# An encoder kernel of two batches: the SBUF slots of each size in pools of their own, at multiples of 256 bytes or more

## The chip, the cores and the metric

The kernel runs on one core of one Trainium2 chip. Its engines are TensorE (PE in the profile, with PEld for the loading of its weights), VectorE (DVE), ScalarE (ACT), GpSimd (POOL) and SyncE (SP), which here issues DMAs. SBUF is the memory on the core, 128 partitions side by side; an address below is a byte offset within a partition, the same in all of them. The metric is the device time of one execution in microseconds, the median of several runs.

## The reference

One layer of an encoder runs over two batches of rows, `x_prompt` (512 rows) and `x_sample` (1024 rows) of 1024 channels, with the same weights, all in float32:

```
h = rmsnorm(x);  z = h @ w_in                       # 1024 x 1792: q, k, v, two conv halves
A = windowed attention(q, k, v)                      # 8 heads of 64, 2 for k and v, |q - k| <= 128, bias, sink
c = ca * sigmoid(cb);  c = dwconv31(c);  c = silu(layernorm(c))
x = x + concat(A, c) @ w_out                         # 1024 x 1024
h = rmsnorm(x);  u = dwconv3(h @ w_up)               # 1024 x 5632
x = x + (silu(u[:, :2816]) * u[:, 2816:]) @ w_down   # 2816 x 1024
y = rmsnorm(x)
```

The outputs are `y_prompt` and `y_sample`, float32.

## The kernel before

Every float32 product is made of fp32r matmuls. An operand is split into a high part (a copy rounded to fp32r, on ACT) and a low part (the operand less the high part, on POOL or DVE), and a product adds three matmuls: high by high, high by low and low by high. Nearly all of them have 128x128 weights and 512 moving columns, so that the moving operand is 2048 bytes in each partition and the weights are 512.

The stages follow each other: transposes and the combined projection (`proj`, lines L299, L300 and L302, one for each of the three matmuls of a product), with the 31-tap convolution beside it on DVE (L354), then attention (L575 for the scores), the output projection, and from about 790 us on the gated MLP for both batches at once. Its up projection and its down projection each save products by a scheme with seven in place of eight, which adds and subtracts blocks ahead of them. The up projection is `prod` (L1079, L1080, L1081), the down projection `mm_down` (L1413, L1414, L1415). The order of instructions on SP and PE is written out by hand in the last part and set by a scheduler before that; no part of it depends on addresses.

All working tiles lie in slots. `Slots` is given classes of slots by a letter: 15 `q` slots of 4096 bytes, 61 `h` of 2048, 4 `c` of 4224, 2 `d` of 2176 and 32 `s` of 64. A request takes the first free slot of the smallest class that fits and gives it back when its tile goes. Where no slot under 4096 bytes is free, a `q` slot is cut into two halves. A slot is a tag of the tile pool `big`: the pool gives a tag its place in SBUF when the tag is first used, and the size that the first tile of the tag has, a multiple of 32 bytes. So the slots lie in the order of their first use, and the sizes are mixed. A second `Slots`, `raws` (L1018), holds the raw weights of the up projection in `q` slots that the first one has handed over.

Where the slots begin in the program as it is built:

```
before   q0 20640, q1 to q5 24736 to 41120, q6 to q14 86432 to 119200
         h0 18592, h1 45280, h2 47392, h3 49504, h4 to h20 51616 to 84384,
         h21 to h27 123296 to 135584, h28 to h32 139808 to 148000, h33 150112, h34 152224, h35 154336,
         h36 to h53 158624 to 193440, h54 195552, h55 197664, h56 199776, h57 to h60 201888 to 208032
         d0 137632, d1 156384, c0 210272, c1 214560, c2 218784, c3 223008
```

Modulo 256, all `q` slots begin at 160, of the `h` slots 48 at 160, h1, h35 and h54 at 224, h2, h28 to h32 and h55 at 32, and h3, h33 and h56 at 96, d0 at 160 and d1 at 224, c0 at 96, c1 and c3 at 32 and c2 at 160. Every slot begins at 32 or 96 past a multiple of 128. Parts of a slot that a matmul reads begin at multiples of 512 bytes within it, so they keep the slot's place modulo 256, the one that the prediction calls an operand's place. Of the 6196 fp32r matmuls, 4416 have weights and moving operand both at 160, and 1780 have one of the two (or both) at 32, 96 or 224. The constants, among them the identity matrix for the transposes, lie in a pool of their own ahead of the slots.

The slots are set up in these lines, which the change replaces or extends:

```
big = ctx.enter_context(tc.tile_pool(name="big", bufs=1))
sb = Slots(big, dict(q=(15, 4096), c=(4, 4224), h=(61, 2048), d=(2, 2176), s=(32, 64)), "q", KEEP)
raws = Slots(big, {})
```

Of the kernel before, what the change touches and what calls it, by code (L numbers as in the profile page):

```python
# [9 lines left out]
F32 = mybir.dt.float32  # L10
# [5 lines left out]
P = 128  # L16
# [40 lines left out]
KEEP = 3  # L57
# [3 lines left out]
U0 = 2  # L61


class Slots:


# [10 lines left out]
    def tile(self, shape, dt=F32, nbytes=4, among=None):  # L77
        need = nbytes
        for s in shape:
            need *= s  # L80
        fits = [s for s in self.free if s[1] >= need and (among is None or s[0][0] in among)]
        if self.halved and nbytes == 4 and need <= 2048 and not any(s[1] < 4096 for s in fits):
            halves = self.halves[dt]
            if not halves and sum(s[0][0] == self.halved for s in fits) > self.keep:
                slot = next(s for s in fits if s[0][0] == self.halved)
                self.free.remove(slot)
                self.n += 1
                whole = Whole(self, slot, dt, self.pool.tile([P, 2, 512], dt, tag=slot[0], name=f"{slot[0]}_{self.n}", bufs=1))
                halves += [(whole, 0), (whole, 1)]
                whole = None  # L90
            if halves:
                return Half(*halves.pop(0), shape)
        if not fits:
            raise RuntimeError(f"no slot for {need} bytes")
        least = min(s[1] for s in fits)
        slot = next(s for s in fits if s[1] == least)
        self.free.remove(slot)
        self.n += 1
        return Held(self, slot, (self.pool(slot[0]) if callable(self.pool) else self.pool).tile([P] + list(shape), dt, tag=slot[0], name=f"{slot[0]}_{self.n}", bufs=1))
# [46 lines left out]
def tile_hybrid_encoder(ctx: ExitStack, tc: tile.TileContext, xs, rel_bias, norm_attn_g, w_in,  # L146
                        attn_sink, conv_dw_w, conv_dw_b, conv_ln_g, conv_ln_b, w_out, norm_ffn_g,
                        w_up, ffn_dw_w, ffn_dw_b, w_down, norm_final_g, onehot, outs):
    nc = tc.nc
    cst = ctx.enter_context(tc.tile_pool(name="cst", bufs=1))  # L150
    big = ctx.enter_context(tc.tile_pool(name="big", bufs=1))
    dr = ctx.enter_context(tc.tile_pool(name="dr", bufs=1, space=bass.MemoryType.DRAM))
    ps_guards = [tc.tile_pool(name=f"ps{i}", bufs=1, space=bass.MemoryType.PSUM) for i in range(4)]
    ps = [guard.__enter__() for guard in ps_guards]
    two_of = dict(a0=0, a1=0, a2=1, u0=1, u1=2, b0=2, b1=3, c0=3)

    sb = Slots(big, dict(q=(15, 4096), c=(4, 4224), h=(61, 2048), d=(2, 2176), s=(32, 64)), "q", KEEP)
    banks = Slots(lambda tag: ps[two_of[tag]], dict(a=(3, 2048), u=(2, 2048), b=(2, 2048), c=(1, 2048)))
    use = dict(step="aub", turn="aub", conv="c", attn="au", norm="b", out="b", up="u", down="b")

# [43 lines left out]
    raws, ws = {}, {}  # L204
# [810 lines left out]


    uraw, third_sum, ops, done = {}, {}, {}, set()
    raws = Slots(big, {})  # L1018

    def reserve(n):  # L1020
        for slot in [s for s in sb.free if s[0][0] == "q"][:n]:
# [636 lines left out]
```

## Time and profile before

| | |
|---|---|
| median of 3 runs | 1562.92 us (1562.15 to 1564.94) |
| profiled execution, from its first to its last instruction | 1559.5 us |
| granted clock of TensorE, mean | 0.990 |
| PE busy | 1505.8 us, 6843 matmuls |
| PEld busy | 1228.9 us |
| DVE busy | 1126.9 us |
| ACT busy | 795.2 us |
| POOL busy | 709.7 us |
| moved by DMA | 227.17 MB, 45.6% of the 16 DMA engines' time |

The page gives the profiled execution's span and no other time of its own. A matmul's duration in the profile runs from its start to the end of its last column's way through the array, so that it is longer than the distance to the start of the next one, and a busy PE is not the same as a PE at its peak. How fast PE goes is read from the distance between starts. In names such as `w<-h,q` the letters are the slot classes: a result in a PSUM bank called `w` from a moving operand in an `h` slot and weights in a `q` slot, or in half of one.

### The profile page before, as it was taken

To read this page: it belongs to the slowest core of one execution; us is meant where nothing else is said; L and a number is where in the kernel's file an instruction comes from. 1 tells how busy PE (TensorE), PEld (TensorE's weight loads), DVE (VectorE), ACT (ScalarE), POOL (GpSimd) and SP (SyncE) were. 2 spreads that over 40 slices of the span, in tenths; PEclk is the share of its full clock that TensorE was granted. 3 is DMA by queue.
4 is the path that set the end of the run, shared out by engine and by line. 5 is a ranking of instruction groups with operands and counts; after the bars stand their busy time and mean duration, and the time that the engine had idled before them with its cause. 6 is when DMAs were issued, how large, how long until landed. Compare 5 with 4: busy or idle time off the path is not lost. (4 is left out here: it accounts for less than half of the span.)

```text
span 1559.5 us, 20112 instructions
## 1 busy us (share of the span) xinstructions
PE 1505.8 (97%) x6843; PEld 1228.9 (79%) x6843; DVE 1126.9 (72%) x1604; ACT 795.2 (51%) x1404; POOL 709.7 (46%) x566
## 2 busy tenths in 40 slices
PE   8998998899999999899999999999999999999997
PEld 6787787787888888777777888888888788888885
DVE  7999767858789785334868777777776845569883
ACT  4634654335787786623455445554545543444354
POOL 6652343226666775947434555555544000003355
PEclk9999999899999999999999999999999999999999
DMA  7582334447344346779332333333332582357644
GB/s 229 157 212 78 108 99 124 128 131 226 111 132 130 117 130 182 241 235 305 108 95 75 102 101 102 102 102 102 102 115 75 191 280 82 105 166 233 220 132 162
DMA packets 228780, 227.17 MB, mean 146 GB/s; under 512 B 13268, under 2 KB 168348, under 8 KB 228549
## 3 DMA queue, kind: packets, MB, share of 16 engines
q1 hardware_dynamic: 228677, 225.88, 45.6%
q8 instruction: 54, 0.88, 0.2%
q14 instruction: 49, 0.40, 0.1%
HBM read 164.74 MB, written 62.14 MB: 145 GB/s over the span
## 5 line engine op out<-in xcount | busy, mean ns | idle before, releaser
L193 POOL TENSOR_TENSOR q<-q,q 128x1024 fp32r<-128x1024 f32 x72 | 173.3, 2414 | 93.5 <-ACT q L192 36.7
L955 POOL TENSOR_TENSOR q<-q,q 128x512 fp32r<-128x512 f32 x101 | 140.7, 1398 | 163.8 <-ACT q L1065 151.5
L955 DVE TENSOR_TENSOR h<-h,h 128x512 fp32r<-128x512 f32 (+2 forms) x202 | 158.4, 817 | 66.2 <-ACT h L959 26.1
L1413 PE MATMUL w<-h,h 128*128 128x512 f32 x462 | 181.4, 393 | 0.5 <-DVE q L1200 0.5
L1414 PE MATMUL w<-h,h 128*128 128x512 f32 x462 | 181.5, 393 | 0.0
L1415 PE MATMUL w<-h,h 128*128 128x512 f32 x462 | 181.1, 392 | 0.0
L1079 PE MATMUL w<-h,q 128*128 128x512 f32 x448 | 176.4, 394 | 3.0 <-ACT w L1171 1.6
L1081 PE MATMUL w<-h,q 128*128 128x512 f32 x448 | 175.5, 392 | 1.0 <-POOL q L955 1.0
L1080 PE MATMUL w<-h,q 128*128 128x512 f32 x426 | 166.5, 391 | 0.0
L299 PE MATMUL u<-h,q 128*128 128x512 f32 x400 | 161.1, 403 | 5.0 <-DVE h L852 4.2
L300 PE MATMUL u<-h,q 128*128 128x512 f32 x400 | 158.9, 398 | 0.0
L302 PE MATMUL u<-h,q 128*128 128x512 f32 x384 | 152.2, 396 | 2.7 <-POOL q L193 2.7
L952 POOL TENSOR_TENSOR q<-q,q 128x1024 f32<-128x1024 f32 x12 | 33.1, 2769 | 238.1 <-DMA h<-gb 197.4
L354 DVE SCALAR_TENSOR_TENSOR c<-c,cvw,c 128x512 f32<-128x512 f32 x184 | 137.9, 750 | 2.9
L959 ACT CAST h<-h 128x512 fp32r<-128x512 f32 x120 | 71.8, 619 | 95.9 <-DVE h L955 42.5
L299 PE MATMUL b<-h,q 128*128 128x512 f32 x256 | 102.3, 400 | 2.7 <-DVE d L384 1.9
L1413 PEld LDWEIGHTS w<-h,h 128*128 128x128 f32 x462 | 86.8, 188 | 20.7 <-ACT h L959 0.9
L1415 PEld LDWEIGHTS w<-h,h 128*128 128x128 f32 x462 | 86.7, 188 | 19.7
L852 DVE SCALAR_TENSOR_TENSOR h<-u,fw,h 128x511 f32<-128x511 f32 x88 | 65.4, 744 | 50.8 <-ACT h L856 50.1
L1414 PEld LDWEIGHTS w<-h,h 128*128 128x128 f32 x462 | 86.8, 188 | 19.4
L1079 PEld LDWEIGHTS w<-h,q 128*128 128x128 f32 x448 | 84.2, 188 | 22.5 <-ACT w L1171 2.1
L302 PE MATMUL b<-h,q 128*128 128x512 f32 x256 | 101.3, 396 | 0.0
(417 smaller groups left out, 3680.3 us busy)
## 6 DMA issues: line engine op xcount, KB each, us to landing
q<-in_w_up SPq DMA_DIRECT2D x88, 512.0 KB
ga<-q SPq DMA_DIRECT2D x64, 256.0 KB
h<-ga SPq DMA_DIRECT2D x57, 256.0 KB
q<-in_w_in SPq DMA_DIRECT2D x28, 512.0 KB
h<-in_w_down SPq DMA_DIRECT2D x52, 256.0 KB
q<-in_x_sample SPq DMA_DIRECT2D x15, 512.0 KB
h<-qsd SPq DMA_DIRECT2D x24, 256.0 KB
x1d<-q SPq DMA_DIRECT2D x11, 512.0 KB
```

Of the source, the lines that this page charges most:

```text
L193: (nc.vector if dve else nc.gpsimd).tensor_tensor(lo[:], raw[:], hi[:].bitcast(F32), op=ALU.subtract)
L299: nc.tensor.matmul(out, whi[:, kc, :], hi[:], start=(kc == 0), stop=False)
L300: nc.tensor.matmul(out, whi[:, kc, :], lo[:], start=False, stop=False)
L302: nc.tensor.matmul(out, wlo[:, kc, :], hi[:], start=False, stop=(kc == KC - 1))
L354: nc.vector.scalar_tensor_tensor(acc[:], src(t), w(t), acc[:], op0=ALU.mult, op1=ALU.add)
L955: (eng or nc.vector).tensor_tensor(out, a, b, op=ALU.subtract)
L1079: nc.tensor.matmul(out, whi[:, s], hi[:], start=(start and c == 0), stop=False, **go)
L1080: nc.tensor.matmul(out, whi[:, s], lo[:], start=False, stop=False, **go)
L1081: nc.tensor.matmul(out, wlo[:, s], hi[:], start=False, stop=(stop and c == 3), **go)
L1413: nc.tensor.matmul(out, sh[:, c], th[:], start=(p == 0), stop=False)
L1414: nc.tensor.matmul(out, sh[:, c], tl[:], start=False, stop=False)
L1415: nc.tensor.matmul(out, sl[:, c], th[:], start=False, stop=(p == NPAIR - 1))
```

## The change

The pool `big` becomes four: `small` for the `s` slots, `full` for the `q` slots, `big` for the `h` slots and `odd` for `c` and `d`. They lie in SBUF in this order behind the constants. A tile `fill` of 216 floats (864 bytes), which nothing uses, is the first thing in `small`, ahead of the `s` slots; with it the `q` slots begin at 20480. The slots of the `odd` pool get their place and size ahead of use, by a first tile of 576 floats (2304 bytes, `d`) or 1088 floats (4352 bytes, `c`). What `Slots` itself knows of sizes stays, so each request gets the slot that it got before.

```diff
+FILL = 216
...
-                whole = Whole(self, slot, dt, self.pool.tile([P, 2, 512], dt, tag=slot[0], name=f"{slot[0]}_{self.n}", bufs=1))
+                whole = Whole(self, slot, dt, (self.pool(slot[0]) if callable(self.pool) else self.pool).tile([P, 2, 512], dt, tag=slot[0], name=f"{slot[0]}_{self.n}", bufs=1))
...
+    small = ctx.enter_context(tc.tile_pool(name="small", bufs=1))
+    full = ctx.enter_context(tc.tile_pool(name="full", bufs=1))
     big = ctx.enter_context(tc.tile_pool(name="big", bufs=1))
+    odd = ctx.enter_context(tc.tile_pool(name="odd", bufs=1))
...
-    sb = Slots(big, dict(q=(15, 4096), c=(4, 4224), h=(61, 2048), d=(2, 2176), s=(32, 64)), "q", KEEP)
+    homes = dict(q=full, h=big, c=odd, d=odd, s=small)
+    small.tile([P, FILL], F32, name="fill")
+    for tag, n in (("d0", 576), ("d1", 576), ("c0", 1088), ("c1", 1088), ("c2", 1088), ("c3", 1088)):
+        odd.tile([P, n], F32, tag=tag, name=f"{tag}_0", bufs=1)
+    sb = Slots(lambda tag: homes[tag[0]], dict(q=(15, 4096), c=(4, 4224), h=(61, 2048), d=(2, 2176), s=(32, 64)), "q", KEEP)
...
-    raws = Slots(big, {})
+    raws = Slots(full, {})
```

Where the slots begin in the program as it is then built:

```
after    q0 to q14 20480 to 77824, h0 to h60 81920 to 204800
         d0 206848, d1 209152, c0 211456, c1 215808, c2 220160, c3 224512
```

All `q` slots begin at multiples of 4096, all `h` slots at multiples of 2048, and `c` and `d` at multiples of 256, so that of the 6196 fp32r matmuls all have both operands at 0 modulo 256. The `s` slots lie from 19456 on. Both programs have the same 13140 instructions, in the same order on every engine, with the same waits, semaphores and queues; only addresses differ.

## The prediction

> **What bounds the kernel now.** I read the page first (span, busy shares, slices), then busy time by stretches, then what TensorE waits for, and last the start times of single matmuls.
>
> The page's head, and its rows for TensorE (PE) and its clock in 40 slices:
>
> ```profile
> span 1559.5 us, 20112 instructions
> PE 1505.8 (97%) x6843; PEld 1228.9 (79%) x6843; DVE 1126.9 (72%) x1604; ACT 795.2 (51%) x1404; POOL 709.7 (46%) x566
> PE   8998998899999999899999999999999999999997
> PEclk9999999899999999999999999999999999999999
> ```
>
> PE is busy 97% of the span at nearly full clock, and nobody else comes near. The view of busy time by stretches (stretch, length, then busy time and instructions touched for PE, weight load, DVE, ACT and POOL, granted clock, DMA share, GB/s) shows how tight that is:
>
> ```profile
> 0.00:60.00 60.00, 51.46 (x250) 41.17 (x251) 48.15 (x67) 31.56 (x49) 40.31 (x58) 0.97 0.67 215
> 95.00:115.20 20.20, 20.20 (x91) 16.73 (x90) 17.98 (x27) 8.82 (x14) 10.97 (x6) 1.00 0.82 208
> 240.00:300.00 60.00, 51.16 (x227) 40.99 (x226) 43.45 (x71) 30.69 (x60) 22.43 (x17) 0.91 0.54 154
> 657.30:661.80 4.50, 4.50 (x12) 3.52 (x11) 0.00 (x0) 0.00 (x0) 4.50 (x4) 0.50 0.52 175
> 1260.00:1490.00 230.00, 230.00 (x1000) 187.47 (x999) 152.79 (x193) 88.47 (x148) 31.39 (x12) 1.00 0.54 177
> 1440.00:1500.00 60.00, 60.00 (x262) 48.87 (x261) 50.61 (x54) 21.77 (x39) 19.46 (x7) 1.00 0.71 236
> 1500.00:1560.00 60.00, 47.89 (x208) 38.61 (x206) 30.69 (x34) 29.06 (x70) 36.79 (x48) 0.94 0.29 109
> sum 1560.00, PE 1505.83 PEld 1228.86 DVE 1126.94 ACT 795.21 POOL 709.74; mean PE 57.92 PEld 47.26 DVE 43.34 ACT 30.58 POOL 27.30
> ```
>
> From 1260 to 1490 us PE is never idle. Of the 26 stretches of 60 us into which the trace is cut, 12 are of that kind (60.00 of 60, the one at 1440 is shown); the three loosest are the first, the one at 240 and the last (shown too). The sum at the end is that of all 26. The waits of PE that are longest in sum are small change:
>
> ```profile
> PE u L299 <- DVE h L852: 4.2, 2, 3.5
> PE u L702 <- DVE q L696: 4.0, 1, 4.0
> ```
>
> So the end is set by how many matmuls PE has and how far apart they start. The change leaves their number, so **all turns on the spacing of matmuls**, of which 6004 are 512-column fp32r ones (128 of 384 and 64 of 256 columns are the rest of the kind).
>
> **The spacing before.** In the 1260 to 1490 stretch the count takes in two matmuls already under way at its start; 230.00/998 is 230.5 ns each. Over all 5823 pairs of such matmuls that start less than 260 ns apart the starts in the trace give 230.1 ns, which is what I use. The stretch at 95 us is faster, and here every operand, weights and moving data, lies 160 bytes past a multiple of 256. Its run in the timeline (start, duration, line, tile), first and last:
>
> ```profile
> 94.06 0.39 PE L300 MATMUL b<-h,q 128*128 128x512 f32 x1
> ...
> 115.39 0.39 PE L302 MATMUL b<-h,q 128*128 128x512 f32 x1
> ```
>
> 94 intervals in 21.33 us: 226.9 ns. It isn't the stage that is fast: two groups of one loop, one behind the other, differ as well. In the first all operands are at 160; in the second one moving operand is in h54 (at 224) and one in h30 (at 32):
>
> ```profile
> 864.94 0.39 PE L1079 MATMUL w<-h,q 128*128 128x512 f32 x1
> ...
> 866.98 0.40 PE L1079 MATMUL w<-h,q 128*128 128x512 f32 x1
> ...
> 867.68 0.40 PE L1079 MATMUL w<-h,q 128*128 128x512 f32 x1
> ...
> 869.78 0.39 PE L1079 MATMUL w<-h,q 128*128 128x512 f32 x1
> ```
>
> Nine intervals each: 2.04 us or 226.7 ns, and 2.10 us or 233.3 ns. The duration of one says the same by group (mean ns after the bar's busy time): 389 where all is at 160, 393 and 394 where a loop meets some other slots:
>
> ```profile
> L300 PE MATMUL b<-h,q 128*128 128x512 f32 x15 | 5.8, 389 | 0.0
> ...
> L1414 PE MATMUL w<-h,h 128*128 128x512 f32 x462 | 181.5, 393 | 0.0
> L1079 PE MATMUL w<-h,q 128*128 128x512 f32 x448 | 176.4, 394 | 3.0 <-ACT w L1171 1.6 <-ACT h L1162 1.1 <-ACT w L1153 0.3
> ```
>
> So spacing follows the address modulo 256, and above all whether it changes from one operand to the next. 1780 of the 6196 fp32r matmuls have an operand at 32, 96 or 224. They pay, and so do their neighbours. In the changed program all 6196 have both operands at 0.
>
> Does even the best run carry something? Here PE ran at half clock (0.50 in the stretch at 657.30, above):
>
> ```profile
> 657.25 0.63 PE L300 MATMUL u<-h,q 128*128 128x512 f32 x1
> ...
> 661.52 0.61 PE L302 MATMUL u<-h,q 128*128 128x512 f32 x1
> ```
>
> Ten intervals in 4.27 us: 427 ns, which halved is 213.5. The best run at full clock has 226.7 to 226.9: some 13 ns more, nearly a sixteenth. No operand of the trace lies at 0, 64 or 128 past a multiple of 256 (all are 32 or 96 past a multiple of 128), so the trace doesn't say whether these 13 ns come from the address.
>
> **The change, part by part.** No instruction, wait, queue or order differs, so there is nothing to sum on ACT, POOL and SP, and FILL and the first tiles of the odd pool issue nothing.
>
> *Other engines' reads.* DVE's largest group reads the same shape from q slots (all at 160 before) and from d slots (160 and 224) at tap offsets 4 bytes apart:
>
> ```profile
> L354 DVE SCALAR_TENSOR_TENSOR c<-d,cvw,c x78: 736/756/757, 41.2 to 166.2; 128x512 f32<-128x512 f32 x78
> L354 DVE SCALAR_TENSOR_TENSOR c<-q,cvw,c x26: 744/756/756, 106.4 to 133.9; 128x512 f32<-128x512 f32 x26
> ```
>
> Both medians are 756 ns: nothing here. *DMA.* Slots that start at multiples of 256 might be written or read in fewer pieces. No row shows such a transfer. It could matter where an engine waits for DMA; the largest of these waits on the way of the first transposes are
>
> ```profile
> 4.65 1.06 ACT L245 ACTIVATE h<-q 128x1024 bf16<-128x1024 f32 x1 [2.44 <-DMA q<-in_x_prompt]
> 8.61 1.06 ACT L245 ACTIVATE h<-q 128x1024 bf16<-128x1024 f32 x1 [2.81 <-DMA q<-in_x_prompt]
> ```
>
> Bounds: a gain of both, 5 us, or as much lost. I take 0, since a start that waits 2 us for a first transfer waits for its way more than for its size, and put it into the range.
>
> *The matmuls.* The price of a uniform phase 0 isn't in the trace. Bounds: 213.5 ns (the half-clock row, halved) and 233.3 ns (the mixed group). The nearest row is the other uniform phase, 226.9 ns at best and settled; I take that. Per matmul 230.1 - 226.9 = 3.2 ns; times 6004 is 19.2 us, and a proportional 0.5 us for the 192 shorter ones: 19.7 us less PE time. How much reaches the end? 12 of the 26 stretches have no idle PE at all and hand on everything; in the other 14 PE has 1505.8 - 720 = 785.8 us of 840, 94%, and there the waits for DVE, ACT or DMA grow when PE comes early; I let 70% through. 0.46 x 1 + 0.54 x 0.7 = 0.84. 19.7 x 0.84 = 16.5 us. The same matmuls that were late are then early for DVE: next behind PE is DVE with 50.61 of 60 us at 1440, so it still has room.
>
> The profiled execution spans 1559.5 us, so the span would be 1543.0. The median of the runs, 1562.92, is 3.4 above this span, which I keep: **1546.4 us**, 1.06% less.
>
> **The rivals.**
>
> *The last 13 ns go too.* If an unaligned row costs one piece more, an aligned one doesn't. For it: the excess in the best run is a sixteenth of a row's time and vanishes at half clock, as if memory needed 17 pieces of 13.3 ns for a row of 2048 bytes that begins inside a piece, where 16 make 213.3. Against it: a fixed cost between two matmuls would also read so, and no aligned operand shows it. Then 230.1 - 213.5 = 16.6 ns x 6004 = 99.7, with the short ones 102 us of PE time. Since DVE has 50.61 of 60 us in the tight stretch above, PE would be held up sooner; I let 80% through: 82 us, 1481 us, and 1470 to 1495 with 70 to 90%. The Trainium skill ("TensorE: Matmul & The Clock Gate", section "Wait — 56ns, not 53.3ns?") gives 215.7 ns start to start for 512 columns at full clock and exactly 426.7 at half clock. The half-clock rows agree; the best full-clock run here, 226.7, doesn't, and by the page's figure an estimate of the saving would be 14.4 x 6004 x 0.8 = 69 us.
>
> *Part of the 13 ns goes*, because weights and moving rows each give up a piece and only one of the two is what PE waits for: 220 ns, 10.1 x 6004 = 61 us, 82% of it 50: 1513 us.
>
> *Nothing happens.* Spacing could follow which operand follows which, by slot, rather than the phase: then 1562.9. The Trainium skill (same page, section "Step-by-step: what each phase is for") says that weights are read through a port of their own and take nothing from the running matmul, by which addresses of the two could not disturb each other. The two groups at 864.94 and 867.68 speak against it: same loop, same shapes, 6.6 ns apart.
>
> *Slower: 0 is a bad phase.* If weights and moving data that begin at the same multiple of 2048 meet in one bank of memory, each matmul is spaced as in the mixed group: 233.3 - 230.1 = 3.2 ns x 6004 = 19.2 us, of which 84% reach the end: 1579 us. It decides as soon as spacing in long runs is over 230.1. For it: in the rows above a phase other than 160 is always the slower. Against it: those are never uniform, so they show the change of phase, not the phase.
>
> **How the numbers follow.** Measurements of this kernel tell 0.2% (3.1 us) from no change. Uniform phase like the best run: 0.44 (its own range 1541 to 1551, by 60 to 100% let through and the DMA bounds). The whole 13 ns: 0.27. Part of it: 0.08. Nothing: 0.07. Slower: 0.14. Faster is the sum of the first three, 0.79. The range leaves out the slower case and the best ends of the 13 ns case: 1472 to 1564.
>
> **What the profile after would show.** As forecast: the run that begins at 94 us keeps 226.7 ns, the second group behind 867 drops from 233.3 to 227, the L1414 group's mean falls from 393 to 389, the stretch from 1260 on counts 1014 matmuls in 230 us in place of 998. If the 13 ns go, even the first of these runs falls to 213 to 216 ns and its duration to about 376; PE idle grows, with waits for DVE at L299 and for ACT at L1079. If 0 is bad, the run at 94 us rises to 233. If DVE's 756 or the first two DMA waits change, what I put at nothing was wrong. The forecast is wrong if all runs are uniform and yet not alike, or if more than 30% of what PE gains turns up as its waits.

## The result and the profile after

The changed kernel takes 1547.56 us (median of 6 runs, 1543.61 to 1548.86), the kernel before 1562.54 us (median of 6, 1558.36 to 1564.94): a ratio of 0.9903 with a 95% interval from 0.9886 to 0.9919, or 15 us less. Timed once more beside another kernel, it came to 0.9905 (0.9888 to 0.9922). The line numbers named here are higher by 10 in the changed kernel: L299 became L309, L1079 became L1089 and L1414 became L1424.

The head of the page after, with the rows for TensorE:

```profile
span 1544.4 us, 20112 instructions
...
PE 1490.0 (96%) x6843; PEld 1227.7 (79%) x6843; DVE 1126.2 (73%) x1604; ACT 795.5 (52%) x1404; POOL 710.7 (46%) x566
...
PE   8899998999999999899999999999999999999996
...
PEclk9999999899999999999999999999999999999998
```

PE is busy for 15.8 us less with the same 6843 matmuls, and the span is shorter by 15.1 us. DVE, ACT and POOL are within 1.0 us of their busy times before. PE's idle time is 54.4 us (1544.4 - 1490.0) and was 53.7. So the gain came out of matmuls that PE does one behind the other, and little of it was lost to waits. Busy time by stretches, in the columns that the prediction explains:

```profile
0.00:60.00 60.00, 50.12 (x250) 39.72 (x251) 48.02 (x67) 31.34 (x49) 40.76 (x58) 1.00 0.65 215
95.00:115.20 20.20, 20.20 (x91) 16.71 (x90) 19.00 (x28) 8.26 (x13) 10.98 (x6) 1.00 0.73 208
960.00:1020.00 60.00, 60.00 (x266) 49.72 (x265) 48.32 (x48) 31.12 (x46) 33.59 (x24) 1.00 0.32 106
1260.00:1490.00 230.00, 230.00 (x1016) 190.44 (x1016) 162.40 (x205) 91.39 (x157) 33.90 (x13) 1.00 0.53 172
1440.00:1500.00 60.00, 60.00 (x266) 49.67 (x265) 53.57 (x52) 25.67 (x51) 29.75 (x15) 1.00 0.62 209
```

From 1260 to 1490 us, 1016 matmuls in place of 1000 find room, and PE still never rests. The stretch at 95 us has 91 as before: it was at its best already. The same in starts of single matmuls, first the run that all lay at 160 before, then the group that was mixed:

```profile
94.15 0.40 PE L310 MATMUL b<-h,q 128*128 128x512 f32 x1
...
115.50 0.39 PE L312 MATMUL b<-h,q 128*128 128x512 f32 x1
```

```profile
862.04 0.39 PE L1089 MATMUL w<-h,q 128*128 128x512 f32 x1
...
864.08 0.39 PE L1089 MATMUL w<-h,q 128*128 128x512 f32 x1
```

94 intervals in 21.35 us are 227.1 ns (before 226.9), and the nine of the second group are 2.04 us or 226.7 ns (before 233.3). From each 512-column fp32r matmul to the fp32r matmul that follows it, where they start under 260 ns apart (some 5730 pairs in each trace), the mean spacing fell from 230.1 to 227.4 ns. This **mean spacing**, taken in the same way, is the measure for the experiments: it hardly moves with waits, and the two layouts of which two traces exist gave 227.4 and 227.5 ns (the changed kernel) and 227.3 and 227.3 ns (all slots at 160, below), while a kernel's time varies by 0.3 to 0.4% from run to run.

By groups (busy time, mean ns):

```profile
L1424 PE MATMUL w<-h,h 128*128 128x512 f32 x462 | 179.7, 389 | 0.0
L1089 PE MATMUL w<-h,q 128*128 128x512 f32 x448 | 175.0, 391 | 2.9 <-ACT w L1181 1.2 <-ACT h L1172 1.2 <-ACT w L1163 0.4
```

393 became 389 and 394 became 391. PE's longest waits hardly differ from before:

```profile
PE u L309 <- DVE h L862: 4.3, 2, 3.5
PE u L712 <- DVE q L706: 4.0, 1, 4.0
PE b L309 <- DVE d L394: 3.0, 1, 3.0
```

The third was 1.9 us; it is the one where PE, now early, waits longer for the convolution on DVE.

### The profile page after: what moved, and what is told of

It is laid out like the page before. It is cut to its first block, busy times and chain, and to the rows that moved or that the text cites. A ratio compares the mean times of both kernels' runs of the same rounds, so it can differ in the third digit from the quotient of the medians.

```text
span 1544.4 us, 20112 instructions
## 1 busy us (share of the span) xinstructions
PE 1490.0 (96%) x6843; PEld 1227.7 (79%) x6843; DVE 1126.2 (73%) x1604; ACT 795.5 (52%) x1404; POOL 710.7 (46%) x566
## 3 DMA queue, kind: packets, MB, share of 16 engines
q1 hardware_dynamic: 228677, 225.88, 45.3%
## 5 line engine op out<-in xcount | busy, mean ns | idle before, releaser
L965 DVE TENSOR_TENSOR h<-h,h 128x512 fp32r<-128x512 f32 (+2 forms) x202 | 153.8, 795 | 65.0 <-ACT h L969 24.4
L1423 PE MATMUL w<-h,h 128*128 128x512 f32 x462 | 179.8, 389 | 0.6 <-DVE q L1210 0.6
L1425 PE MATMUL w<-h,h 128*128 128x512 f32 x462 | 179.7, 389 | 0.0
L1424 PE MATMUL w<-h,h 128*128 128x512 f32 x462 | 179.7, 389 | 0.0
L1089 PE MATMUL w<-h,q 128*128 128x512 f32 x448 | 175.0, 391 | 2.9 <-ACT w L1181 1.2
L309 PE MATMUL u<-h,q 128*128 128x512 f32 x400 | 159.4, 399 | 5.2 <-DVE h L862 4.3
L962 POOL TENSOR_TENSOR q<-q,q 128x1024 f32<-128x1024 f32 x12 | 33.8, 2823 | 233.3 <-DMA h<-gb 194.4
L309 PE MATMUL b<-h,q 128*128 128x512 f32 x256 | 102.3, 400 | 4.0 <-DVE d L394 3.0
L1423 PEld LDWEIGHTS w<-h,h 128*128 128x128 f32 x462 | 86.7, 188 | 19.1 <-ACT h L969 1.0
L1089 PEld LDWEIGHTS w<-h,q 128*128 128x128 f32 x448 | 84.2, 188 | 21.4 <-ACT w L1181 1.6
L312 PE MATMUL b<-h,q 128*128 128x512 f32 x256 | 101.0, 395 | 0.0
L310 PE MATMUL b<-h,q 128*128 128x512 f32 x256 | 101.0, 394 | 0.0
L1425 PEld LDWEIGHTS w<-h,h 128*128 128x128 f32 x462 | 86.7, 188 | 18.0
```

The lines of the kernel that those rows point to most:

```text
L309: nc.tensor.matmul(out, whi[:, kc, :], hi[:], start=(kc == 0), stop=False)
L310: nc.tensor.matmul(out, whi[:, kc, :], lo[:], start=False, stop=False)
L312: nc.tensor.matmul(out, wlo[:, kc, :], hi[:], start=False, stop=(kc == KC - 1))
L965: (eng or nc.vector).tensor_tensor(out, a, b, op=ALU.subtract)
L1089: nc.tensor.matmul(out, whi[:, s], hi[:], start=(start and c == 0), stop=False, **go)
L1423: nc.tensor.matmul(out, sh[:, c], th[:], start=(p == 0), stop=False)
```

## The experiments

The theory: what the change gave is one place modulo 256 bytes for all fp32r operands, not the multiple of 256. The rival: an operand at a multiple of 256 is read faster in its own right. Below them lies a second question: which places have to agree, those of one moving operand and the next, or those of weights and moving operand.

**All slots at 160.**

```diff
-FILL = 216
+FILL = 256
```

> All slots moved up by 160 bytes together (FILL of 256 floats): every fp32r operand at 160 modulo 256, none at a multiple of 64. If what the change gave is one place modulo 256 for all operands: mean spacing of 512-column matmuls 227.4 ns as after the change, span 1544 us, time 0.990 of before. If it gave the multiple of 256 itself: back to about 230 ns, span 1559 us, ratio 1.00.

Mean spacing 227.3 ns, ratio 0.9922 (0.9898 to 0.9945), span 1547.0 us. In the long stretch:

```profile
1260.00:1490.00 230.00, 230.00 (x1017) 190.65 (x1015) 161.34 (x202) 90.06 (x153) 33.51 (x12) 1.00 0.54 174
```

No operand lies at a multiple of 64 here, and PE is as fast as after the change. For TensorE, then, the rival falls. What is left of it is in the time, and comes below.

**Every second h slot 32 bytes on.**

```diff
+late_h = ctx.enter_context(tc.tile_pool(name="late_h", bufs=1))
+late_h.tile([P, 8], F32, name="shift")
-sb = Slots(lambda tag: homes[tag[0]], ...)
+sb = Slots(lambda tag: late_h if tag[0] == "h" and int(tag[1:]) % 2 else homes[tag[0]], ...)
```

The `c` and `d` slots, which lie behind the `h` slots, move on by 32 bytes with them.

> The changed kernel with every second h slot 32 bytes on: of 6004 512-column matmuls 2929 begin with a moving operand at another place modulo 256 than the one before (before: 1980, after: 0), and in 3148 weights and moving operand differ (before: 1664). The change saved 2.65 ns x 6004 = 15.9 us, that is 8.0 us per 1000 changes of the moving operand or 9.6 us per 1000 differing pairs. If changes from one moving operand to the next cost: 23.5 us over the changed kernel, mean spacing 231.3 ns, span 1568 us. If differing pairs cost: 30 us, 232.4 ns, span 1574 us. If operands that aren't at a multiple of 256 cost (3826 matmuls have one, 6004 before): 10 us, span 1554 us.

Mean spacing 231.75 ns, more than before the change, with PE busy for 1513.6 us. The long stretch counts 994 matmuls, where the changed kernel has 1016 and the kernel before 1000:

```profile
1260.00:1490.00 230.00, 230.00 (x994) 186.25 (x993) 149.38 (x192) 87.08 (x146) 26.43 (x10) 1.00 0.53 174
```

Against the changed kernel that is 4.3 ns x 6004 = 26 us, between the two first expectations and far from the third. The time is 1.0015 of before (1.0002 to 1.0029), the median 1566.9 us. 32 bytes on half of the slots take away all that the change gave. This layout can't tell whether the step from one moving operand to the next costs or the pair; the next two bear on that.

**Every second q slot 32 bytes on (weights), the h slots at multiples of 256.**

```diff
+late_q = ctx.enter_context(tc.tile_pool(name="late_q", bufs=1))
+late_q.tile([P, 8], F32, name="shift"); big.tile([P, 56], F32, name="back")
+sb = Slots(lambda tag: late_q if tag[0] == "q" and int(tag[1:]) % 2 else homes[tag[0]], ...)
-raws = Slots(full, {})
+raws = Slots(lambda tag: late_q if int(tag[1:]) % 2 else full, {})
```

> The changed kernel with every second q slot 32 bytes on; the q slots hold nearly always weights here. Moving operands change place at 14 of 6003 steps, weights at 814, and in 1905 matmuls weights and moving operand differ. If only the moving operand's changes cost: as after, 227.4 ns, span 1544 us. If a change of weights costs as much as one of the moving operand (8.0 us per 1000): 6.5 us, 228.5 ns, span 1551 us. If differing pairs cost (9.6 us per 1000): 18 us, 230.5 ns, span 1563 us.

229.6 ns, span 1561.0 us. The moving operands nearly all stay at 0, and still it costs 2.2 ns x 6004 = 13 us: that only the moving operand's changes count is out. 13 us lie between the two other expectations, 6.5 us for changes of weights and 18 us for differing pairs, so this run doesn't decide between them. The starts can be grouped by whether the weights of a matmul, or those of the next one, lie at another place than its moving operand (within runs without a break, their first few intervals left out): both agree, 227.3 ns (some 3370 intervals); only its own differ, 230.3 (some 310); only the next one's differ, 235.8 (some 310); both differ, 233.0 (some 1330).

**All q slots at 160, all h slots at 0.**

```diff
 small.tile([P, FILL], F32, name="fill")
+full.tile([P, 40], F32, name="shift"); big.tile([P, 24], F32, name="back")
```

> The changed kernel with all q slots at 160 modulo 256 and all h slots at 0: weights and moving operand differ in 3500 of 6004 matmuls, but steadily, with 146 changes of place of the moving operand and 221 of the weights. If changes from one matmul to the next cost: 1 to 3 us over the changed kernel, 227.6 to 228 ns, span 1545 to 1547 us. If differing pairs cost: 33 us, 233 ns, span 1578 us, with the loss in the lines with h moving and q weights alone and none in the down projection.

231.2 ns, span 1567.8 us, though hardly any operand's place changes. A stretch of the up projection (moving in h, weights in q) and one of the down projection (both in h) show the two sides in one kernel:

```profile
960.00:1020.00 60.00, 60.00 (x259) 48.42 (x258) 44.87 (x43) 27.71 (x40) 27.04 (x19) 1.00 0.32 104
1260.00:1490.00 230.00, 230.00 (x1017) 190.44 (x1016) 152.62 (x197) 88.86 (x149) 27.78 (x10) 1.00 0.56 183
```

259 where the changed kernel has 266, and 1017 where it has 1016: the loss is where pairs differ, and the down projection, whose pairs agree, has none. So **a lasting difference between weights and moving operand costs**, with hardly a change of place from one matmul to the next. It costs less than I set: 3.7 ns x 6004 = 22 us for 3500 pairs, 6.4 us per 1000 in place of 9.6. The difference is in what a pair that comes and goes does to its neighbours.

In the changed kernel the first ten intervals behind a group of transposes or another break go 233, 232, 232, 229, 230, 231, 228, 229, 229, 227 ns in the mean, and only then stay at 226.7. A differing pair is such a break, too. In the trace of the kernel before, with an interval counted as disturbed where the weights of a matmul or of the next one lie at another place than its moving operand, the undisturbed ones behind a disturbed one go 231, 231, 230, 229, 229, 228, 228 and 227 ns in the mean, and from the ninth on they stay within 0.2 ns of 226.7. Those in a run that has had ten intervals and no differing pair are at 226.7 (435 intervals), as in the changed kernel: what the change took away is the pairs and the matmuls behind them. Pairs that stay find no such rhythm while they last: with q at 160, intervals whose own and next weights both lie elsewhere take 233.4 ns (2889 of them), but few undisturbed ones stand behind a pair.

**q slots 256 and 128 bytes from the h slots.** The q slots are put at 256 modulo 512, or at 128 modulo 256, with the h slots where the changed kernel has them:

```diff
-FILL = 216
+FILL = 152                                  # 184 for 128 bytes
+big.tile([P, 64], F32, name="back")         # 32 for 128 bytes
```

> The changed kernel with all q slots at 256 modulo 512 and all h slots at 0 modulo 512 (both at 0 modulo 256); weights come from q and moving operands from h in all lines but the down projection's. If weights and moving operand must agree modulo 256: as the changed kernel, mean spacing 227.4 ns, span 1544 us. If they must agree modulo 512 or more: as with 160 between them, 231 ns, span 1568 us.

> The changed kernel with all q slots at 128 modulo 256 and all h slots at 0: 3500 of 6004 matmuls have weights and moving operand 128 bytes apart modulo 256. If they must agree modulo 256: as with 160 between them, 231 ns, span 1568 us. If agreeing modulo 128 or 64 is enough: as the changed kernel, 227.4 ns, span 1544 us.

At 256: 227.4 ns, span 1545.2 us. At 128: 230.5 ns, span 1566.7 us. The same stretch of the up projection, 256 first:

```profile
960.00:1020.00 60.00, 60.00 (x266) 49.67 (x266) 48.36 (x48) 31.33 (x47) 34.71 (x24) 1.00 0.32 106
```

```profile
960.00:1020.00 60.00, 60.00 (x260) 48.71 (x259) 45.30 (x44) 28.06 (x41) 27.09 (x19) 1.00 0.33 108
```

So weights and moving operand must agree modulo 256: 128 isn't enough, and agreement modulo 512 isn't needed.

**All slots at 128**, where the identity matrix lies too.

```diff
-FILL = 216
+FILL = 248
```

> All slots moved up by 128 bytes together (FILL of 248 floats): every fp32r operand at 128 modulo 256, where the identity matrix of the transposes lies too. If one place for all is what counts: mean spacing 227.4 ns, span 1544 us. If the slower first ten matmuls after a group of transposes (228 to 233 ns in place of 226.7 in the changed kernel) come from the identity's other place: these go too, 226.7 to 226.9 ns, span 1540 us.

227.35 ns, and the first ten intervals behind a break are 231.5, 232, 233, 229, 230, 230, 228, 228, 228 and 227: the slow start doesn't come from the identity's place. The span is 1549.2 us, PE busy 1489.8.

**Half of the load for two of three matmuls of the down projection.**

```diff
-nc.tensor.matmul(out, sh[:, c], th[:], start=(p == 0), stop=False)
-nc.tensor.matmul(out, sh[:, c], tl[:], start=False, stop=False)
-nc.tensor.matmul(out, sl[:, c], th[:], start=False, stop=(p == NPAIR - 1))
+nc.tensor.matmul(out, sh[:, c], th[:], start=(p == 0), stop=(p == NPAIR - 1), skip_group_check=True)
+nc.tensor.matmul(out[0:64, :], sh[:, c][:, 0:64], tl[:], start=False, stop=False, skip_group_check=True)
+nc.tensor.matmul(out[0:64, :], sl[:, c][:, 0:64], th[:], start=False, stop=(p == NPAIR - 1), skip_group_check=True)
```

> The changed kernel, but two of every three matmuls of the down projection (high by low and low by high, 924 of 1386) use 64 of the 128 columns of their weights, so that half of their correction terms is left out. If the 13 ns that a settled matmul takes over 213.3 are time taken by the load of the next weights from the same memory: intervals in which a halved load runs fall to about 220 ns, the down projection's mean to 222.2, span about 1538 us. If they are a fixed cost between two matmuls or of the moving row: 226.7 everywhere, span 1544 us.

```profile
1260.00:1490.00 230.00, 230.00 (x1004) 152.34 (x1003) 158.54 (x200) 90.03 (x151) 33.06 (x12) 1.00 0.54 173
```

Neither. PEld's busy time falls from 190.44 to 152.34 us, but the matmuls get slower: 1004 in place of 1016. The intervals from L1423 to L1424 are 228.1 ns (227.0 in the changed kernel), L1424 to L1425 231.5 (226.5), L1425 to L1423 228.8 (226.5). Why isn't shown: the edit halves the rows of the result along with the weights that are loaded, and the longest interval, L1424 to L1425, lies between two matmuls of equal load. What the 13 ns over 213.5 are that a settled matmul takes stays open: neither the three common places tried nor half of the load take them away.

**The changed kernel and all slots at 160, timed side by side.**

> The changed kernel once more, timed beside the next one. One place for all is what counts: 0.990 of before, as first measured, and the same as with all slots at 160.

> All slots at 160 modulo 256, timed more closely. One place for all is what counts: within 0.2% of the changed kernel. If multiples of 256 give something more (to DMA, say): 0.2 to 0.4% slower, as the first medians, 1552.32 and 1547.56 us, would have it.

The changed kernel ran in 1546.68 us (5 runs, 1543.83 to 1548.3; 0.9905 of before), the one at 160 in 1550.28 (6 runs, 1549.07 to 1553.38; 0.9933, 0.9916 to 0.995). No run of the one reaches into the range of the other: 3.6 us or 0.23% (4.8 us in the first pair of medians, which were not taken side by side). That is the second expectation, by little: the two intervals of the ratios overlap, and only the ranges of the runs tell the layouts apart. Spacing is the same (227.5 and 227.3 ns). The rows for the engines and for the DMA queue, of the changed kernel and then of the one at 160:

```profile
span 1546.5 us, 20112 instructions
...
PE 1493.0 (97%) x6843; PEld 1230.5 (80%) x6843; DVE 1121.5 (73%) x1604; ACT 795.8 (51%) x1404; POOL 708.4 (46%) x566
...
q1 hardware_dynamic: 228677, 225.88, 45.3%
```

```profile
span 1550.5 us, 20112 instructions
...
PE 1490.0 (96%) x6843; PEld 1227.8 (79%) x6843; DVE 1124.4 (73%) x1604; ACT 795.0 (51%) x1404; POOL 709.5 (46%) x566
...
q1 hardware_dynamic: 228677, 225.88, 46.4%
```

PE has 60.5 us of idle time at 160 and 53.5 in the changed kernel (57.2 and 54.4 in the first traces of the two), and the same packets take 46.4% of 1550.5 us, 719 us, against 45.3% of 1546.5, 701 us. Two other layouts go along: with all slots at 128 the queue's time is 717 us and PE's idle time 59.4, with q at 256 it is 703 and 53.8. Over all the traces here the queue's time is 700 to 707 us where every big slot begins at a multiple of 256 (4 traces), 711 to 719 where none does (6, with the kernel before at 711 and 53.7 us of idle time), and 704 to 714 where some do. So transfers take less time at multiples of 256, by some 2%. That PE's shorter waits come from it is likely, not shown. The Trainium skill ("DMA: Bandwidth & Descriptors", section "How a descriptor splits into AXI transactions") says that a descriptor which doesn't begin at a multiple of 256 bytes costs extra beats. The direction agrees with these rows.

**Parts of the change alone.** From the kernel before, once only the s slots in a pool apart, once only the c and d slots widened and set up first (the first one also has the line by which a pool can be chosen by tag, as in the change):

```diff
+small = ctx.enter_context(tc.tile_pool(name="small", bufs=1))
-sb = Slots(big, ...)
+sb = Slots(lambda tag: small if tag[0] == "s" else big, ...)
```

```diff
+[big.tile([P, n], F32, tag=t, name=f"{t}_0", bufs=1)
+ for t, n in (("d0", 576), ("d1", 576), ("c0", 1088), ("c1", 1088), ("c2", 1088), ("c3", 1088))]
```

> The kernel before with the s slots alone in a pool of their own; c and d slots stay among the others. Weights and moving operand differ modulo 256 in 1076 of 6004 matmuls (before 1664, all slots apart 0), the moving operand's place changes at 880 steps (before 1980). At 9.6 us per 1000 differing pairs: 10 us over the changed kernel, mean spacing 229.1 ns, span 1555 us; at the 4 to 5.5 us per 1000 that the kernels with shifted q slots cost: 4 to 6 us, 228.1 to 228.4 ns, span 1549 to 1551 us.

> The kernel before with the c and d slots alone widened to multiples of 256 bytes and set up first, in the one pool; the s slots stay among the others. Weights and moving operand differ in 1094 matmuls, and the moving operand's place changes at 1515 steps. At 9.6 us per 1000 differing pairs: 10.5 us over the changed kernel, 229.2 ns, span 1555 us; if changes of the moving operand's place counted (8.0 us per 1000): 12 us, 229.4 ns, span 1557 us, and then more than with the s slots apart (7 us, 228.6 ns, span 1551 us).

The s slots apart: 229.05 ns, span 1556.6 us, 1558.41 us in its one run. The widened slots: 229.4 ns, span 1560.0 us, 1561.78 us. The head of each page:

```profile
span 1556.6 us, 20112 instructions
...
PE 1499.9 (96%) x6843; PEld 1228.1 (79%) x6843; DVE 1125.9 (72%) x1604; ACT 795.5 (51%) x1404; POOL 709.4 (46%) x566
```

```profile
span 1560.0 us, 20112 instructions
...
PE 1501.3 (96%) x6843; PEld 1227.1 (79%) x6843; DVE 1125.3 (72%) x1604; ACT 795.6 (51%) x1404; POOL 709.1 (45%) x566
```

Of the 2.65 ns that the whole change takes off, the one gives 1.0 and the other 0.65: less than two thirds together. A few tiles out of place spoil the rhythm for many. With the s slots apart, some 9 us per 1000 differing pairs came out, near the first expectation (9.6 us, 229.1 ns); the 4 to 5.5 us of the other expectation were too low, since the kernels with shifted q slots cost 5.3 to 6.9. The widened slots came out at the value expected for changes of the moving operand's place (229.4 ns). The two kernels have nearly the same number of differing pairs (1076 and 1094), but 880 and 1515 changes of the moving operand's place, and the one with more changes is slower by 0.4 ns. So the number of pairs doesn't set the price alone. That it matters how often they come and go, too, fits the settling above; no run changes that alone. The widened slots alone took 4.5 us off PE's busy time and nothing off the span; both kernels have all their big slots off the multiples of 256, a queue time of 716 us (46.0% of 1556.6 and 45.9% of 1560.0) and 3 to 5 us more idle time of PE than before. Why their idle time grew stays open, since the big slots of the kernel before are off the multiples of 256 too.

## Why the prediction was right

- *The likeliest case* held: a uniform phase of 0 is as good as the uniform phase of 160, 226.7 ns when settled. 1546.4 us were forecast and 1547.56 measured. The stretch from 1260 us was to count 1014 matmuls beside the two under way, and counts 1016 with them; the mean of the L1414 group was to fall to 389 and did.
- *The term per matmul was too large*: 3.2 ns (230.1 less 226.9) were taken and 2.65 measured, 15.9 us in place of 19.2. The 226.9 ns are those of a long run. The 227.4 that came out hold the first ten intervals behind each break, which none of the placings tried here mended.
- *The share that reaches the end was too small*: 0.84 against 0.95 (15.1 of 15.9 us). The 70% for the 14 looser stretches were a guess. The longest single waits, such as the 4.0 us at L712, hardly grew. The two errors cancel to within 1.4 us: that the sum is so near is in part luck.
- *DMA at 0* was wrong in size, within its 5 us. Timed beside the layout at 160, the multiple of 256 is worth 3.6 us. At 160 PE's busy time falls as far, but less of it comes through: the ratio is 0.9933. So part of the 95% may belong to this term. The start-up waits that I took as its bound were the wrong place to look:

```profile
4.88 1.06 ACT L255 ACTIVATE h<-q 128x1024 bf16<-128x1024 f32 x1 [2.67 <-DMA q<-in_x_prompt]
7.71 1.06 ACT L255 ACTIVATE h<-q 128x1024 bf16<-128x1024 f32 x1 [1.67 <-DMA q<-in_x_prompt]
```

  One is longer by 0.2 us and one shorter by 1.1.
- *DVE at nothing* was right; the medians by slot are 756 ns as before:

```profile
L364 DVE SCALAR_TENSOR_TENSOR c<-d,cvw,c x78: 735/756/758, 41.2 to 164.8; 128x512 f32<-128x512 f32 x78
L364 DVE SCALAR_TENSOR_TENSOR c<-q,cvw,c x26: 747/756/756, 105.5 to 132.7; 128x512 f32<-128x512 f32 x26
```

- *The 13 ns go too*, or a part of them: no. Settled spacing is 226.7 ns at 0, at 128 and at 160. This rival had the half-clock rows for it, which show that the excess goes at half clock but not what it is. Its reading that no operand lay at 128 past a multiple of 256 holds for the fp32r matmuls alone: the identity matrix of the transposes lay there.
- *Nothing happens*: no. Its page ("TensorE: Matmul & The Clock Gate", section "Step-by-step: what each phase is for", in the Trainium skill) has weights and moving data on ports of their own. The runs don't fit a reading by which the two can't disturb each other: with q at 160 and h at 0, the up projection is slower by 3% (259 against 266 matmuls in 60 us) for nothing but a difference between the two addresses.
- *0 is a bad phase*: no. What stood for it, that each phase but 160 was slower, came from their being the rare ones.
- The prediction spoke of spacing that depends "above all" on whether the address "changes from one operand to the next". That was too loose: between one moving operand and the next no change is needed; weights and moving operand at different places are enough. That changes make it worse holds as far as they bring differing pairs that come and go.

## What to carry to other kernels

Where matmuls run back to back on fp32r operands, look at the starts of single matmuls, not only at the busy share: a PE that is 97% busy still lost 1% to where its tiles lay. Put the tiles that hold weights and those that hold moving data at the same place modulo 256 bytes, and small or odd-sized tiles into a pool of their own, so that one of them can't shift all that follow; of the common places tried, 0, 128 and 160 served TensorE alike, and at 0 the transfers took less time as well. A step worth single nanoseconds is measured by the mean spacing of one trace, which told apart kernels whose times overlapped.

## What was not expected of the hardware

- Two operands of TensorE disturb each other by their addresses modulo 256: 227.4 ns mean spacing with 0 or 256 bytes between them, 230.5 with 128 and 231.2 with 160 between them in three fifths of the matmuls.
- In the kernels with q at 160 or alternating by 32, the next matmul's weights weigh more than its own (235.8 against 230.3 ns with q alternating, 234.3 against 230.3 with q at 160). That fits the timeline, where the load of the next weights starts with a matmul (both at 899.90 us in the changed kernel, for one). With 128 bytes between them it is even, though (232.1 and 232.2). So which load meets the moving data isn't settled.
- After a break, the spacing takes about ten matmuls to settle to 226.7 ns, from 233 ns with all slots at 0 and from 231 to 233 at 128 and 160; behind a differing pair it takes about as many, from 231.
- Halving the weight columns of two matmuls in three, and with them the rows of their results, made the matmuls slower, by 1 to 5 ns each; why is open.
